# Low-weight products issued one key block later, and one product for both rotated halves of the sliding keys

## The chip, the cores and the metric

The kernel runs on one core of one Trainium2 chip. The metric is the device time of one execution in microseconds (us), from the first to the last instruction with what lies around them; it was 3167.22 us in the median of three runs. Five engines work side by side and wait for each other through semaphores: TensorE (PE: matrix products; PEld is its loading of the stationary operand), VectorE (DVE), ScalarE (ACT), GpSimd (POOL) and SyncE (SP, which starts the DMA transfers).

## The reference

Two transformer blocks run one after the other on 2048 tokens of width 1024, in float32. The parts that matter here are three attentions, each with 8 heads of width 64:

```python
# first block, heads 0-7: causal, with a forget gate
s = q @ k.T * scale + cum[q] - cum[k]; p = softmax(where(causal, s, -inf)); o = p @ v
# first block, heads 8-15: sliding window of 128 with a sink, two key heads, rotary positions
q, k = rope(q), rope(k); s = q @ k.T * scale; p = softmax(concat(where(band, s, -inf), sink)); o = p[:, :-1] @ v
# second block: 16 meta keys, and for each query its 256 best keys by an index score
s = q_lat @ c.T * scale + bias; p = softmax(where(selected, s, -inf)); o = p @ c
# rope: halves x1, x2 of a head
concat([x1 * cos - x2 * sin, x2 * cos + x1 * sin])
```

Around them stand the input projections, gates, a recurrent layer (HGRN2) beside the third attention, output projections and norms.

## The kernel before, in words

**Products in halves.** A float32 factor is split into a high and a low float16 half. A projection is three products per 128 of the width: high by high, high by low, low by high (`mm3_T`, lines 326 to 328 for a result with tokens along the free axis, `mm3_R`, lines 337 to 339, for tokens along the partitions).

**Attention.** All three attentions are built alike. Queries come in groups of 512 (`g`, four of them), keys in blocks of 128 (`j`). For one head and group, `prepare` loads operands and finds row maxima through extra score products, and `main` gives a list of steps: `block(j)` for each key block up to the diagonal, then `norm`. A block makes the scores, keys along the partitions, in a PSUM tile `pst`; `Att.weights` takes the exponential of it on ScalarE into a float32 tile `p32` (line 746), casts it to the high half `phi` on ScalarE or VectorE (lines 748 and 750) and subtracts to get the low half `plo` on GpSimd, some on VectorE (line 752). Each of these three tiles has three buffers. Then `Att.pv` is called for each 128 queries `s` of the group: the high half by the values' high part with a column of ones (line 776, 65 columns), the high half by the values' low part (line 777, 64 columns), and the low half by the values' high part (line 778). All of it accumulates in one PSUM tile `po` per head and group, which has one buffer. `norm` divides and stores. The sliding attention has two blocks per head and group; the last attention has one more, `meta`, for the 16 meta keys, with weights in the tiles `wmhi` and `wmlo`.

**Order.** `weave` lays the steps of `main` between those of the next head's `prepare`. The order of the text isn't the order on the engines: when the program is built, a planner with a model of times lays out each engine's queue, and takes what is earlier in the text first where it thinks it ready, with shifts from `tc.high_priority`. What writes to one PSUM tile stays in the order of the text. On the chip each engine then works through its queue.

**Projections of the first block.** `stream` goes through the weight blocks of `blocks1`; the heads' attention is woven in. `rotated` handles queries and keys of the sliding attention, whose weight columns are ordered so that the first halves of the heads come first. For each group of 512 tokens it makes one product for the first halves and one for the second halves (`m` rows each: 128 for four query heads, 64 for the two key heads), each in one of the two PSUM buffers `pp`, multiplies both by cosine and sine on VectorE (lines 523 and 524), combines on GpSimd (line 525), splits and stores. The work tiles `ra` have four buffers.

Of the kernel before, what the change touches and what calls it, by code (L numbers as in the profile page):

```python
# [10 lines left out]
F32 = mybir.dt.float32  # L11
# [456 lines left out]
def blocks1(K, A, h, sp, wp, er, ps, pso, fa, cum):  # L468

    nc = K.nc  # L470
# [33 lines left out]
    def rotated(kind, c0, m):  # L504
        def f(w, inv, rn):
            q, k, c, ci = (x[:, c0:c0 + 1] for x in (K.sq, K.sk, K.sc_, K.sci))
            if kind == "kb":
                angles(K, A, sp)
                norm_scale(K, wp, rn, K.hn, k)
                nc.vector.tensor_copy(K.sk[:, 1:2], k)  # L510
                inv = times(K, wp, "inv8", inv, k)
            else:
                norm_scale(K, wp, rn, times(K, wp, "hn8", K.hn, 8.0), q)
                score_scale(K, q, k, c, ci)
                inv = times(K, wp, "inv8", inv, 0.125, q)
            for g in range(NG):
                p = [ps.tile([128, 512], F32, name="pp")[:m] for _ in range(2)]
                for a in range(2):
                    mm3_T(K, p[a], w, a * m, h[g])
                tb = [table(g, a)[:m] for a in range(2)]  # L520
                for a in range(2):
                    x, y = (sp.tile([128, 512], F32, name="ra", tag="ra", bufs=4)[:m] for _ in range(2))
                    nc.vector.scalar_tensor_tensor(x, p[a], inv[:m], tb[0], op0=ALU.mult, op1=ALU.mult)  # L523
                    nc.vector.scalar_tensor_tensor(y, p[1 - a], inv[:m], tb[1], op0=ALU.mult, op1=ALU.mult)
                    nc.gpsimd.tensor_tensor(x, x, y, op=ALU.add if a else ALU.subtract)
                    store_rot(x, halves_of(K.d_qb, c0 * 4, 4, a, g * 512, 512) if kind == "qb" else
                              halves_of(K.d_kb, 0, 2, a, g * 512, 512))
        return f
# [46 lines left out]
    for kind, c0, cols in BLK1:  # L575
        n = sum(m for _, m in cols)
# [145 lines left out]
class Att:  # L722
# [46 lines left out]
        nc.scalar.copy(qa[64:66], p[64:66])  # L769
        return z  # L770

    def pv(self, o, hi, lo, v, first=False, last=False):

        nc = self.K.nc
        kw = dict(skip_group_check=True)
        nc.tensor.matmul(o, lhsT=hi, rhs=v[:, :65], start=first, stop=False, **kw)  # L776
        nc.tensor.matmul(o[:, 1:65], lhsT=hi, rhs=v[:, 65:129], start=False, stop=False, **kw)  # L777
        nc.tensor.matmul(o, lhsT=lo, rhs=v[:, :65], start=False, stop=last, **kw)  # L778

    def norm(self, po, inv, h, dst, add=None, key="on"):  # L780

# [21 lines left out]
class Swa:  # L803
# [62 lines left out]
    def main(self, g, h, ops):  # L866
        K, at = self.K, self.at
        nc = K.nc
        QA, QB, es = ops
        KA, KB, v = self.keys[g, h // 4]  # L870

        def scores(p, c, j, s, n, mask, m0):
            k, q = slice(j * 128, j * 128 + 128), slice(s * 128, s * 128 + n)
            kw = dict(skip_group_check=True)
            nc.tensor.matmul(p[:, c:c + n], lhsT=KA[:66, k], rhs=QA[:66, q], start=True, stop=False, **kw)
            nc.tensor.matmul(p[:, c:c + n], lhsT=KB[:, k], rhs=QB[:, q], start=False, stop=False, **kw)
            nc.tensor.matmul(p[:, c + m0:c + n], lhsT=K.idb, rhs=mask, start=False, stop=True, **kw)

        po = []

        def block(b):
            if b == 0:
                po.append(self.pso.tile([128, 4, 65], F32, name="spo"))
            p = self.pst.tile([128, 512], F32, name="pst")
            if b == 0:

                scores(p, 128, 4, 3, 128, K.mT2[:, :128], 0)
                if g:
                    scores(p, 0, 0, 0, 128, K.mT2[:, 128:], 0)
                scores(p, 256, 1, 0, 256, K.mT2, 0)  # L890
                prods = [(1, 4, 3), (2, 1, 0), (3, 1, 1)] + ([(0, 0, 0)] if g else [])
            else:
                scores(p, 0, 2, 1, 256, K.mT2, 0)
                scores(p, 256, 3, 2, 256, K.mT2, 0)
                prods = [(0, 2, 1), (1, 2, 2), (2, 3, 2), (3, 3, 3)]
            cc = 128 if b == 0 and g == 0 else 0
            hi, lo = at.weights(p[:, cc:], K.sci[:, h // 4:h // 4 + 1])
            for i, (c, j, s) in enumerate(prods):
                c = slice(c * 128 - cc, c * 128 - cc + 128)
                at.pv(po[0][:, s], hi[:, c], lo[:, c], v[:, j], first=b == i == 0)  # L900

        def norm():
            at.norm(po[0], K.vinvb[:, h // 4:h // 4 + 1], h, o_rows(K.d_o, D, g, 512 + h // 2 * 128), add=es, key="son")

        return [lambda: block(0), lambda: block(1), norm]


def phase_first(K, A, sk):
# [4 lines left out]
    with ExitStack() as st, ExitStack() as sr:  # L913
# [59 lines left out]
        def main(g, h, ops):  # L973
            KA, KB, QA, QB, v = ops
            po = pso.tile([128, 4, 65], F32, name="po")

            def block(j):
                s0 = max(0, j - 4 * g)
# [6 lines left out]
                if diag:  # L985
                    nc.tensor.matmul(p[:, s0 * 128:s0 * 128 + 128], lhsT=K.idb, rhs=K.mT, start=False, stop=True)
                hi, lo = at.weights(p[:, c0:], K.fci[:, h // 4:h // 4 + 1])
                for s in range(s0, 4):
                    c = slice((s - s0) * 128, (s - s0) * 128 + 128)
                    at.pv(po[:, s], hi[:, c], lo[:, c], v[:, j], first=j == 0 and s == 0, last=j == 4 * g + s)  # L990

            def norm():
                at.norm(po, K.vinv[:, h:h + 1], h, o_rows(K.d_o, D, g, h // 2 * 128), key=f"on{g % 2}")

            return [lambda j=j: block(j) for j in range(4 * g + 4)] + [norm]
# [982 lines left out]
def phase_dsa(K, A, out):  # L1978

    nc, tc = K.nc, K.tc  # L1980
    with ExitStack() as st:
# [97 lines left out]

        def main(g, h, ops, mk):  # L2080
            KA, KB, QA, QB, v, bT, bM = ops
            n = (g + 1) * 512
            po = pso.tile([128, 4, 65], F32, name="po")
            def meta():

                p = pst.tile([128, 512], F32, name="pst")
                nc.tensor.matmul(p, lhsT=KA[:66, :128], rhs=QA[:66], start=True, stop=False)
                nc.tensor.matmul(p, lhsT=KB[:, :128], rhs=QB, start=False, stop=g > 0)
                if g == 0:
                    for a in range(2):  # L2090
                        nc.tensor.matmul(p[:, :256], lhsT=jr, rhs=bM[:, a], start=False, stop=a == 1)
                hi, lo = wm
                at.weights(p[:16], K.dci[:, h // 4:h // 4 + 1], (hi, lo))
                for s in range(4):
                    c = slice(s * 128, s * 128 + 128)
                    at.pv(po[:, s], hi[:, c], lo[:, c], v[:, 0], first=s == 0)

            def block(j):
                s0 = max(0, j - 4 * g)
# [17 lines left out]
                for s in range(s0, 4):  # L2117
                    c = slice((s - s0) * 128, (s - s0) * 128 + 128)
                    at.pv(po[:, s], hi[:, c], lo[:, c], v[:, j + 1], last=j == 4 * g + s)

            def norm():
                pc = sm.tile([128, 4, 65], F32, name="pc", bufs=1)
                nc.scalar.copy(pc, po)
                at.norm(pc, K.vinv[:, h:h + 1], h, o_rows(K.d_a, D, g, h // 2 * 128), key="on")
# [209 lines left out]
```

## Time and profile before

| what | us |
|---|---|
| median of three runs | 3167.22 |
| lowest and highest | 3156.71, 3170.61 |
| profiled execution, its own time | 3170.48 |
| its span, first to last instruction | 3168.7 |
| TensorE busy in it | 2822.7 |

Times in the rows are microseconds unless marked ns. A row of a group of instructions has line, engine, operation, what it writes <- reads, shapes and count, then busy time, mean duration of one in ns, idle time of its engine just before, and what ended most of that idle time. Records of matrix products overlap, since a product's record holds the way through the array; the distance between two starts tells what one takes of the engine. TensorE's granted clock was 0.938 of the full 2.4 GHz in the mean. The first block's projections and attentions run to about 1400 us, the second block's projections and index scores to about 2240 us, and the last attention with the recurrent layer and the output projection from there to the end.

### The profile page before, as it was taken

The numbers are of one execution on the slowest core, as the hardware profiler recorded it, in microseconds if no ns is written. First come the engines' busy times: TensorE is split into PE (matmuls) and PEld (weight loads), VectorE is DVE, ScalarE is ACT, GpSimd is POOL, SyncE is SP. The second block draws the span as 40 slices with busy tenths as digits, with TensorE's granted clock in tenths as the row PEclk, the third lists the DMA queues.
The fourth block names the chain that finished last, engine by engine and source line by source line (L and its number), as shares of the span: only waits on it lengthen the run. The fifth ranks groups of instructions, "written<-read, shape, count | busy, mean of one in ns | idle before, by whom it ended". The sixth has DMA issues, their size and how long they took to land. (4 is left out here: it accounts for less than half of the span.)

```text
span 3168.7 us, 65862 instructions
## 1 busy us (share of the span) xinstructions
PE 2822.7 (89%) x25152; PEld 1858.8 (59%) x25152; DVE 2101.6 (66%) x5073; ACT 1686.9 (53%) x3058; POOL 1450.2 (46%) x1241
## 2 busy tenths in 40 slices
PE   7899999999997899999998889899678888988997
PEld 5554444477884555544445665358566566666663
DVE  7523765566678676646499699830578778888763
ACT  4423665576566655634356466321455456657763
POOL 3211446564333555534233433610456567768752
PEclk9899999999996799999999989899679989999998
DMA  6222343532235343334433532222753444443331
GB/s 235 82 87 84 105 129 111 173 95 69 79 94 167 109 142 108 124 91 157 111 97 101 160 125 73 89 91 63 182 159 102 137 133 113 118 117 110 122 97 59
DMA packets 271184, 364.28 MB, mean 115 GB/s; under 512 B 60205, under 2 KB 192033, under 8 KB 269705
## 3 DMA queue, kind: packets, MB, share of 16 engines
q1 hardware_dynamic: 270424, 359.96, 37.8%
q8 instruction: 199, 3.26, 0.4%
q14 instruction: 129, 1.05, 0.1%
q10 hardware_dynamic: 432, 0.02, 0.0%
HBM read 247.05 MB, written 112.82 MB: 114 GB/s over the span
## 5 line engine op out<-in xcount | busy, mean ns | idle before, releaser
L752 POOL TENSOR_TENSOR plo<-p,phi 128x512 f16<-128x512 f32 (+3 forms) x600 | 664.9, 1121 | 569.9 <-ACT phi L748 360.0
L748 ACT CAST phi<-p 128x512 f16<-128x512 f32 (+3 forms) x649 | 347.0, 554 | 84.2 <-PE po L778 75.1
L746 ACT ACTIVATE p<-pst,shift,dci 128x512 f32<-128x512 f32 (+4 forms) x352 | 247.4, 716 | 137.2 <-POOL plo L752 46.7
L778 PE MATMUL po<-v,plo 128*128 128x65 f16 x2176 | 270.1, 196 | 35.0 <-POOL plo L752 27.9
L776 PE MATMUL po<-v,phi 128*128 128x65 f16 x2176 | 286.4, 197 | 5.3 <-ACT phi L748 4.2
L777 PE MATMUL po<-v,phi 128*128 128x64 f16 x2176 | 285.3, 198 | 0.0
L778 PEld LDWEIGHTS <-plo 128*128 128x128 f16 x2424 | 234.7, 101 | 79.2 <-POOL plo L752 46.8
L746 ACT ACTIVATE p<-pst,shift,fci 128x512 f32<-128x512 f32 (+1 forms) x320 | 220.1, 710 | 113.1 <-PE pst L984 70.2
L963 DVE TENSOR_REDUCE mu<-p 128x1 f32<-128x512 f32 (+2 forms) x320 | 188.4, 603 | 130.1 <-PE p L959 83.3
L776 PEld LDWEIGHTS <-phi 128*128 128x128 f16 x2424 | 236.1, 100 | 48.8 <-ACT phi L748 11.4
L284 POOL TENSOR_TENSOR wlo<-wraw,whi 128x512 f16<-128x512 f32 (+3 forms) x116 | 149.9, 1310 | 216.9 <-ACT whi L283 214.0
L2058 DVE CUSTOM_DVE_ANT_0 jk<-p,mk 128x512 bf16<-128x512 f32 (+2 forms) x320 | 193.4, 604 | 80.5 <-PE p L2052 32.8
L777 PEld LDWEIGHTS <-phi 128*128 128x128 f16 x2424 | 235.6, 100 | 15.3 <-issue 1.8
L337 PE MATMUL pp<-whi,hhi 128*128 128x256 f16 (+2 forms) x824 | 235.0, 286 | 7.7 <-ACT whi L283 5.7
L339 PE MATMUL pp<-whi,hlo 128*128 128x256 f16 (+2 forms) x824 | 233.2, 285 | 4.2 <-POOL hlo L465 4.2
L338 PE MATMUL pp<-wlo,hhi 128*128 128x256 f16 (+2 forms) x824 | 234.7, 285 | 0.6 <-POOL wlo L284 0.6
L326 PE MATMUL pp<-hhi,whi 128*128 128x512 f16 (+2 forms) x496 | 190.7, 384 | 4.4 <-DVE ra L523 4.4
L328 PE MATMUL pp<-hhi,wlo 128*128 128x512 f16 (+2 forms) x496 | 190.3, 384 | 0.0
L327 PE MATMUL pp<-hlo,whi 128*128 128x512 f16 (+2 forms) x496 | 190.0, 383 | 0.0
L328 PEld LDWEIGHTS <-wlo 128*128 128x128 f16 (+2 forms) x1000 | 99.7, 100 | 122.6 <-POOL wlo L284 10.9
L326 PEld LDWEIGHTS <-whi 128*128 128x128 f16 (+2 forms) x1000 | 100.5, 101 | 120.1 <-issue 10.2
L327 PEld LDWEIGHTS <-whi 128*128 128x128 f16 (+2 forms) x1000 | 99.9, 101 | 117.3 <-issue 16.0
(666 smaller groups left out, 8933.6 us busy)
## 6 DMA issues: line engine op xcount, KB each, us to landing
wraw<-in_w_in_dram SPq DMA_DIRECT2D x88, 256.0 KB
d_z<-er SPq DMA_DIRECT2D x128, 128.0 KB
bT<-d_rb SPq DMA_DIRECT2D x32, 384.0 KB
wa<-in_w_ada_dram SPq DMA_DIRECT2D x8, 1024.0 KB
x<-in_x_dram SPq DMA_DIRECT2D x16, 512.0 KB
d_k<-ehi SPq DMA_DIRECT2D x32, 256.0 KB
d_q<-ehi SPq DMA_DIRECT2D x32, 256.0 KB
QA<-d_q SPq DMA_DIRECT2D x64, 128.0 KB
```

The costliest lines, as they stand in the source:

```text
L326: nc.tensor.matmul(ps, lhsT=whi, rhs=hhi[:, kk, :], start=kk == 0, stop=False)
L327: nc.tensor.matmul(ps, lhsT=whi, rhs=hlo[:, kk, :], start=False, stop=False)
L328: nc.tensor.matmul(ps, lhsT=wlo, rhs=hhi[:, kk, :], start=False, stop=kk == KK - 1)
L337: nc.tensor.matmul(ps, lhsT=hhi[:, kk, s], rhs=whi, start=kk == 0, stop=False)
L338: nc.tensor.matmul(ps, lhsT=hhi[:, kk, s], rhs=wlo, start=False, stop=False)
L339: nc.tensor.matmul(ps, lhsT=hlo[:, kk, s], rhs=whi, start=False, stop=kk == KK - 1)
L746: nc.scalar.activation(p, s, AF.Exp, scale=ci[:m], bias=K.shift[:m])
L748: nc.scalar.copy(hi, p)
L752: e.tensor_tensor(lo, p, hi, op=ALU.subtract)
L776: nc.tensor.matmul(o, lhsT=hi, rhs=v[:, :65], start=first, stop=False, **kw)
L777: nc.tensor.matmul(o[:, 1:65], lhsT=hi, rhs=v[:, 65:129], start=False, stop=False, **kw)
L778: nc.tensor.matmul(o, lhsT=lo, rhs=v[:, :65], start=False, stop=last, **kw)
```

## The change

Two things change. In `rotated`, where a half has 64 rows (the sliding keys), one product of 128 rows makes both halves; a copy on ScalarE brings rows 64 to 127 to a tile of partitions 0 to 63. In the attentions, `pv` is called once per block with all its products: it issues the products of the high weights for all query columns, then those of the low weights of the block before, which it finds in the list `late`, and puts its own low products there. `flush`, at the start of `norm`, issues what is left.

```diff
             for g in range(NG):
-                p = [ps.tile([128, 512], F32, name="pp")[:m] for _ in range(2)]
-                for a in range(2):
-                    mm3_T(K, p[a], w, a * m, h[g])
+                if m == 64:
+
+                    pb = ps.tile([128, 512], F32, name="pp")
+                    mm3_T(K, pb, w, 0, h[g])
+                    z = sp.tile([128, 512], F32, name="ra", tag="ra", bufs=4)[:m]
+                    nc.scalar.copy(z, pb[m:])
+                    p = [pb[:m], z]
+                else:
+                    p = [ps.tile([128, 512], F32, name="pp")[:m] for _ in range(2)]
+                    for a in range(2):
+                        mm3_T(K, p[a], w, a * m, h[g])
...
-    def pv(self, o, hi, lo, v, first=False, last=False):
+    def pv(self, prods, late):
+
 
         nc = self.K.nc
         kw = dict(skip_group_check=True)
-        nc.tensor.matmul(o, lhsT=hi, rhs=v[:, :65], start=first, stop=False, **kw)
-        nc.tensor.matmul(o[:, 1:65], lhsT=hi, rhs=v[:, 65:129], start=False, stop=False, **kw)
-        nc.tensor.matmul(o, lhsT=lo, rhs=v[:, :65], start=False, stop=last, **kw)
+        for o, hi, lo, v, first, last in prods:
+            nc.tensor.matmul(o, lhsT=hi, rhs=v[:, :65], start=first, stop=False, **kw)
+            nc.tensor.matmul(o[:, 1:65], lhsT=hi, rhs=v[:, 65:129], start=False, stop=False, **kw)
+        self.flush(late)
+        late.append(lambda: [nc.tensor.matmul(o, lhsT=lo, rhs=v[:, :65], start=False, stop=last, **kw)
+                             for o, hi, lo, v, first, last in prods])
+
+    def flush(self, late):
+        while late:
+            late.pop(0)()
...
                 hi, lo = at.weights(p[:, c0:], K.fci[:, h // 4:h // 4 + 1])
-                for s in range(s0, 4):
-                    c = slice((s - s0) * 128, (s - s0) * 128 + 128)
-                    at.pv(po[:, s], hi[:, c], lo[:, c], v[:, j], first=j == 0 and s == 0, last=j == 4 * g + s)
+                cs = lambda s: slice((s - s0) * 128, (s - s0) * 128 + 128)
+                at.pv([(po[:, s], hi[:, cs(s)], lo[:, cs(s)], v[:, j], j == 0 and s == 0, j == 4 * g + s)
+                       for s in range(s0, 4)], late)
 
             def norm():
+                at.flush(late)
                 at.norm(po, K.vinv[:, h:h + 1], h, o_rows(K.d_o, D, g, h // 2 * 128), key=f"on{g % 2}")
...
```

The sliding attention and the last one (its `meta` and `block`) are changed in the same way, with a list `late` for each head and group.

## Rows read from the trace of the kernel before

**Rows 1.** The page, part 1: busy time of each engine over the span.

```profile
PE 2822.7 (89%) x25152; PEld 1858.8 (59%) x25152; DVE 2101.6 (66%) x5073; ACT 1686.9 (53%) x3058; POOL 1450.2 (46%) x1241
```

**Rows 2.** Busy time in stretches: PE, PEld, DVE, ACT, POOL, clock, DMA share, GB/s.

```profile
430.00:505.00 75.00, 72.51 (x551) 37.68 (x552) 40.90 (x90) 39.82 (x80) 46.90 (x44) 1.00 0.37 111
...
700.00:950.00 250.00, 246.69 (x2963) 209.85 (x2961) 165.75 (x521) 156.93 (x296) 94.32 (x95) 1.00 0.28 84
...
950.00:1400.00 450.00, 396.52 (x3521) 241.47 (x3520) 301.40 (x757) 262.32 (x473) 217.40 (x175) 0.88 0.41 124
...
2240.00:3168.00 928.00, 790.47 (x9356) 567.10 (x9354) 691.36 (x1430) 542.37 (x902) 579.57 (x453) 0.92 0.41 119
```

**Rows 3.** Groups of PE by shape, 430 to 505 us: count | busy, mean ns.

```profile
L328 PE MATMUL pp<-hhi,wlo 128*64 128x512 f16 x57 | 21.7, 383 | 0.0
...
L328 PE MATMUL pp<-hhi,wlo 128*128 128x512 f16 x11 | 4.2, 379 | 0.0
```

**Rows 4.** Timeline of PE in that stretch: start us, duration us, instruction.

```profile
442.66 0.38 PE L327 MATMUL pp<-hlo,whi 128*64 128x512 f16 x1
...
446.54 0.38 PE L327 MATMUL pp<-hlo,whi 128*64 128x512 f16 x1
```

**Rows 5.** Groups of ACT over the span: the nearest copy out of PSUM.

```profile
L1857 ACT COPY kr<-y 128x512 f32<-128x512 f32 (+1 forms) x16 | 9.3, 579 | 3.9 <-PE y L1855 3.9
```

**Rows 6.** Timeline from 2849.5 us: one wait for a low half.

```profile
2848.75 2.13 POOL L752 TENSOR_TENSOR plo<-p,phi 128x512 f16<-128x512 f32 x1
...
2849.85 0.20 PE L776 MATMUL po<-v,phi 128*128 128x65 f16 x1
...
2850.93 0.20 PE L778 MATMUL po<-v,plo 128*128 128x65 f16 x1 [0.67 <-POOL plo L752]
...
2850.97 0.20 PE L776 MATMUL po<-v,phi 128*128 128x65 f16 x1
```

**Rows 7.** Groups of line 778 in 300:700, then 950:1400, then 2240:3168 (three rows).

```profile
L778 PE MATMUL po<-v,plo 128*128 128x65 f16 x425 | 50.2, 194 | 3.9 <-POOL plo L752 3.5 <-DVE plo L752 0.2
...
L778 PEld LDWEIGHTS <-plo 128*128 128x128 f16 x425 | 40.1, 99 | 12.7 <-POOL plo L752 7.4 <-issue 0.9 <-POOL ehi L481 0.4
...
L778 PEld LDWEIGHTS <-plo 128*128 128x128 f16 x570 | 56.5, 104 | 22.9 <-POOL plo L752 11.4 <-DVE plo L752 4.4 <-POOL z L1058 1.2
...
L778 PE MATMUL po<-v,plo 128*128 128x65 f16 x420 | 53.5, 200 | 7.6 <-POOL plo L752 4.5 <-DVE plo L752 1.5 <-DVE iq L224 1.2
...
L778 PE MATMUL po<-v,plo 128*128 128x65 f16 x1088 | 136.9, 197 | 23.3 <-POOL plo L752 19.7 <-DVE plo L752 3.0
...
L778 PEld LDWEIGHTS <-plo 128*128 128x128 f16 x1088 | 106.2, 102 | 42.0 <-POOL plo L752 27.7 <-DVE plo L752 4.2 <-issue 2.8
...
L778 PE MATMUL po<-v,wmlo 128*128 128x65 f16 x128 | 15.6, 194 | 3.6 <-POOL wmlo L752 3.5
```

**Rows 8.** The chain that ended last, 2242 to 3168 us, by line.

```profile
by line: issue 8.3%; POOL plo L752 4.2%; PE y L1147 4.0%; PE y L1145 4.0%; PE y L1146 3.9%; PE pst L2115 3.9%; PE pst L2103 3.8%; PE pst L2104 3.8%; DVE jk L2058 3.7%; PE p L2052 3.7%; DVE dc L1847 3.3%; DMA raw<-in_w_out_dram 2.7%; PE po L
```

**Rows 9.** Waits, over the span (three rows), then in 2240:3168 (one).

```profile
ACT phi L748 <- PE po L778: 75.1, 70, 5.2
...
ACT p L746 <- POOL plo L752: 57.0, 71, 3.6
...
POOL plo L752 <- PE po L778: 25.5, 17, 3.0
...
ACT p L746 <- POOL plo L752: 46.7, 60, 3.6
```

**Rows 10.** The page, part 5: the steps that make weights, and line 776's loads.

```profile
L752 POOL TENSOR_TENSOR plo<-p,phi 128x512 f16<-128x512 f32 (+3 forms) x600 | 664.9, 1121 | 569.9 <-ACT phi L748 360.0
L748 ACT CAST phi<-p 128x512 f16<-128x512 f32 (+3 forms) x649 | 347.0, 554 | 84.2 <-PE po L778 75.1
L746 ACT ACTIVATE p<-pst,shift,dci 128x512 f32<-128x512 f32 (+4 forms) x352 | 247.4, 716 | 137.2 <-POOL plo L752 46.7
...
L776 PEld LDWEIGHTS <-phi 128*128 128x128 f16 x2424 | 236.1, 100 | 48.8 <-ACT phi L748 11.4
```

More of the change, by code (lines that the diff above doesn't have):

```diff
@@ L877, in scores @@
             nc.tensor.matmul(p[:, c + m0:c + n], lhsT=K.idb, rhs=mask, start=False, stop=True, **kw)
-        po = []
+        po, late = [], []
         def block(b):
@@ L897, in block @@
             hi, lo = at.weights(p[:, cc:], K.sci[:, h // 4:h // 4 + 1])
-            for i, (c, j, s) in enumerate(prods):
-                c = slice(c * 128 - cc, c * 128 - cc + 128)
-                at.pv(po[0][:, s], hi[:, c], lo[:, c], v[:, j], first=b == i == 0)
+            cs = lambda c: slice(c * 128 - cc, c * 128 - cc + 128)
+            at.pv([(po[0][:, s], hi[:, cs(c)], lo[:, cs(c)], v[:, j], b == i == 0, False)
+                   for i, (c, j, s) in enumerate(prods)], late)
         def norm():
+            at.flush(late)
             at.norm(po[0], K.vinvb[:, h // 4:h // 4 + 1], h, o_rows(K.d_o, D, g, 512 + h // 2 * 128), add=es, key="son")
@@ L975, in main @@
             po = pso.tile([128, 4, 65], F32, name="po")
+            late = []
             def block(j):
@@ L987, in block @@
                 hi, lo = at.weights(p[:, c0:], K.fci[:, h // 4:h // 4 + 1])
-                for s in range(s0, 4):
-                    c = slice((s - s0) * 128, (s - s0) * 128 + 128)
-                    at.pv(po[:, s], hi[:, c], lo[:, c], v[:, j], first=j == 0 and s == 0, last=j == 4 * g + s)
+                cs = lambda s: slice((s - s0) * 128, (s - s0) * 128 + 128)
+                at.pv([(po[:, s], hi[:, cs(s)], lo[:, cs(s)], v[:, j], j == 0 and s == 0, j == 4 * g + s)
+                       for s in range(s0, 4)], late)
             def norm():
+                at.flush(late)
                 at.norm(po, K.vinv[:, h:h + 1], h, o_rows(K.d_o, D, g, h // 2 * 128), key=f"on{g % 2}")
@@ L2081, in main @@
             KA, KB, QA, QB, v, bT, bM = ops
-            n = (g + 1) * 512
+            late = []
             po = pso.tile([128, 4, 65], F32, name="po")
@@ L2093, in meta @@
                 at.weights(p[:16], K.dci[:, h // 4:h // 4 + 1], (hi, lo))
-                for s in range(4):
-                    c = slice(s * 128, s * 128 + 128)
-                    at.pv(po[:, s], hi[:, c], lo[:, c], v[:, 0], first=s == 0)
+                cs = lambda s: slice(s * 128, s * 128 + 128)
+                at.pv([(po[:, s], hi[:, cs(s)], lo[:, cs(s)], v[:, 0], s == 0, False) for s in range(4)], late)
             def block(j):
@@ L2116, in block @@
                 hi, lo = at.weights(p[:, c0:], K.dci[:, h // 4:h // 4 + 1])
-                for s in range(s0, 4):
-                    c = slice((s - s0) * 128, (s - s0) * 128 + 128)
-                    at.pv(po[:, s], hi[:, c], lo[:, c], v[:, j + 1], last=j == 4 * g + s)
+                cs = lambda s: slice((s - s0) * 128, (s - s0) * 128 + 128)
+                at.pv([(po[:, s], hi[:, cs(s)], lo[:, cs(s)], v[:, j + 1], False, j == 4 * g + s)
+                       for s in range(s0, 4)], late)
             def norm():
+                at.flush(late)
                 pc = sm.tile([128, 4, 65], F32, name="pc", bufs=1)
```

## The prediction

> **What bounds the kernel now.** I read the page's busy times first. TensorE is busy 89% of the span, its weight loads 59%, and no other engine passes 66% [rows 1]. That 89% isn't a full TensorE: a 65-column product is recorded with 0.20 us, yet the next starts 0.04 us after it (2850.93 and 2850.97, [rows 6]), so the records overlap. So I went on by stretches [rows 2]. The first projections with head attention woven in (430 to 505 us) leave the matmul engine 2.5 of 75 us; from 700 to 950 us it is idle for 3 of 250. From 950 to 1400 it is idle 53 of 450 us, and in the last attention (2240 to 3168) 138 of 928, where VectorE has 691 us of work and GpSimd 580. So TensorE is the bound up to about 950 us, and later stages hang on chains that cross engines.
>
> The wait that the change is about is seen in one block [rows 6]: GpSimd is 2.13 us in writing the low half, TensorE issues the first two high products of the block (line 776, then 777) and then stands until 2850.93 us at line 778, though the high products of the other three column groups need nothing more; they follow 0.04 us later. By stretches, the matmul engine idles at line 778 for 3.9, 7.6 and 23.3 us, and 3.6 us at the sixteen meta keys' one; the weight loads idle longer, 12.7, 22.9 and 42.0 us [rows 7]. The chain that ended last, which covers the last 926 us alone, names the subtraction that makes the low half for 4.2% of them, 39 us [rows 8].
>
> **The sliding keys.** Two 64-row products per group of 512 tokens become one of 128 rows. It removes 4 groups x 24 products = 96 matmuls and their 96 loads. A 64-row product takes as long as a 128-row one, 383 against 379 ns [rows 3], though the records overlap here too: in an unbroken run the eighteenth product after the one at 442.66 us starts at 446.54 [rows 4], so one takes 3.88 / 18 = 0.216 us of the engine. 96 x 0.216 = 20.7 us. The stretch has 2.5 us of idle TensorE, and the stage behind it 3 in 250, so what is saved moves everything behind it: I take the whole, bounds 0 (below, case D) and 20.7.
>
> It adds four copies of 64x512 out of PSUM on ScalarE. The nearest row, 128x512 out of PSUM, has 579 ns [rows 5]: 4 x 0.58 = 2.3 us on an engine that is busy 40 of 75 us there [rows 2]; priced at nothing, 2.3 us if that cover were gone. The copy waits for its group's last product; behind it on ScalarE stand exponentials and casts of the heads, and two of the group's four VectorE products now wait 0.58 us longer, hidden by the two that read the other half straight from PSUM. A product now holds one PSUM buffer instead of both, so the next group's product can begin while VectorE still reads this one; that is worth at most the 2.5 us and I count nothing. Four `ra` buffers now serve five tiles a group: the fifth takes the slot of the copy, whose last reader stands ahead of it on VectorE; nothing.
>
> **The products of the low weights.** No product and no load is added or removed. All high products of a block go first, then the low ones of the block before. In [rows 6] the six high products that stood behind line 778 would have gone at 2849.9. What it is worth lies between nothing (the next wait ends just as late) and the idle time of the loads, 12.7 + 22.9 + 42.0 = 77.6 us. An idle load costs nothing while a product still streams, so I go by the matmul engine's own idle time. Up to 1400 us I take all of it, 3.9 + 7.6 = 11.5 us. In the last attention it is 23.3 + 3.6 = 26.9 us, and of that I take half, 13.4: there GpSimd's subtraction also holds up the exponentials, which wait 46.7 us for it because the float32 weights have three buffers [rows 9], and this the change doesn't touch. So 25 us, bounds 0 and 78.
>
> Two more effects. The buffer of the high half is released by the high products alone, no longer by products that stand behind a low half; ScalarE waits 75.1 us for it, 70 times [rows 9]. I count nothing in the sum, since ScalarE is at 53% [rows 1]; it is case B. At a head's end the lows of the last two blocks now follow its last high product, at most three more products at 0.04 us [rows 6], 0.12 us a head; over 96 heads (eight, in four groups, three times) this is bounded by 12 us. I take nothing: the subtraction of the last block isn't ready sooner, and they run under it.
>
> **A rule that speaks against it.** In [rows 6] the high products that were ready waited behind line 778: products ran in the order in which they were issued. The Trainium skill, page "TensorE: Matmul & The Clock Gate", section "Part 2: What happens when you issue a matmul", says that matmuls stay in program order and that only weight loads are pulled ahead. By that rule the wait may only change its place, from the low half to the next block's high half (case C); the sum would then keep the keys' part alone.
>
> **Sum.** 20.7 + 25 = 45.7 us. The profiled execution took 3170.5 us, 3.3 above the median of the three runs; on the median that gives 3167.2 - 45.7 = 3121.5 us, 1.4% less; a profiled execution would take some 3125. I say 3121.
>
> **The cases.** A difference of about 0.5% (16 us) is what a measurement of this kernel can tell from none.
>
> A (0.50), the sum. For it speaks that the idle time at line 778 is named in every attention stage [rows 7]. Its own range has 8 to 58 us for the lows beside the keys' 20.7: 3088 to 3138.
>
> B (0.15), more than the sum: the waits of ScalarE for the high half's buffer were part of the same chain. If 40 of the 75.1 us come back too, 3121 - 40 = 3081. For it: the two waits occur in the same blocks, since a low half that is late keeps the buffer of the high half. Against: exponentials still wait for GpSimd [rows 9].
>
> C (0.13), the wait moves to the high products. Between blocks that follow each other on ScalarE lie one exponential and one cast, 0.72 + 0.55 = 1.27 us, and the low half comes 1.12 us after its high half [rows 10]: the next high half can be as late as the low half was, and behind it on TensorE are queued the lows, ready by then, and the score products that come after them, on which the next exponential waits. Then the lows give nothing and 3167 - 20.7 = 3146 stays. Against it: of the 48.8 us that loads idle at line 776 only 11.4 are put down to the cast [rows 10], so the order on TensorE mostly comes to the high products once they are ready.
>
> D (0.12), the keys' saving doesn't arrive and the lows give little: at 950 us another stage begins, whose idle time and clock of 0.88 [rows 2] show that it isn't paced by TensorE alone. With 0 to 10 us: 3157 to 3167.
>
> E (0.10), slower. The order is laid out anew by the planner, and each low half's buffer is held until the next block's high products have gone, one block longer: 928 us over 352 exponentials is 2.6 us [rows 2, 10]. There are three buffers. GpSimd waits for them 17 times now, 25.5 us, 1.5 us each [rows 9]. The gain is used up when 31 more such waits lie on the chain (45.7 / 1.5), and from 42 on the kernel is slower by over 16 us; at 47 it is 3167 - 45.7 + 70.5 = 3192. Against: a block's subtraction and its hold come to 1.12 + 2.6 us, of three buffers' 7.9.
>
> Faster by over 0.5%: A, B and most of C, 0.75. Within: the rest of C and D, 0.15. Slower: E, 0.10. The range, 3070 to 3160, takes in A, C, most of B and the low end of D; E lies outside, with the far end of B (lows at their bound of 78: 3069).
>
> **What would show it.** Right: 96 fewer products, none of 128*64 from the sliding keys; the stage behind 700 us begins some 20 us sooner; idle time of the matmul engine at line 778's successor falls from 38 us over the three stretches to under 10, and that of line 776 hardly grows; ScalarE's wait for the high half's buffer falls below 40 us. For C: the cast is named for over 30 us ahead of the high products. For D: the stage at 950 us starts sooner, but ends when it did. For E: GpSimd's wait for the low half's buffer is 70 us or more. Wrong altogether would be a last attention that takes as long as before although line 778 no longer waits: then that wait was not what set the end, and my half of it too much.

## The result, and the profile after

The changed kernel takes 3211.17 us in the median of four runs (3210.18 to 3212.24), the kernel before 3162.06 us in the median of four beside it (3156.71 to 3170.61). The ratio is 1.0152, with a 95% interval of 1.0128 to 1.0176: slower by some 49 us, where 46 us were forecast as gain.

The busy times of the page answer to [rows 1]: TensorE has the 96 products fewer, and 5.6 us less to do, in a span that is 41 us longer.

```profile
PE 2817.1 (88%) x25056; PEld 1854.7 (58%) x25056; DVE 2126.7 (66%) x5073; ACT 1684.6 (52%) x3056; POOL 1440.2 (45%) x1241
```

The windows answer to [rows 2], with the same columns.

```profile
430.00:505.00 75.00, 58.91 (x412) 30.30 (x410) 57.54 (x102) 40.52 (x81) 52.68 (x46) 0.91 0.39 117
...
700.00:950.00 250.00, 246.30 (x2961) 207.41 (x2958) 170.81 (x516) 159.34 (x298) 96.90 (x97) 1.00 0.27 82
950.00:1400.00 450.00, 383.80 (x3450) 234.99 (x3447) 300.82 (x750) 262.24 (x474) 210.50 (x172) 0.88 0.39 118
...
2240.00:3168.00 928.00, 783.49 (x9315) 567.55 (x9313) 678.10 (x1436) 543.45 (x904) 569.27 (x449) 0.90 0.42 120
```

From 430 to 505 us TensorE is busy 58.9 us where it was 72.5, and does 139 products fewer, so more than the 96 that were removed: it isn't ahead, it is idle (16.1 us of the 75). From 950 to 1400 us it does 71 products fewer than before.

The waits over the span answer to [rows 9].

```profile
POOL plo L760 <- PE po L789: 86.7, 50, 7.2
...
PEld L786 <- ACT phi L756: 48.1, 54, 5.3
...
ACT p L754 <- POOL plo L760: 39.1, 45, 3.1
```

GpSimd now waits 86.7 us for a free low-half buffer (25.5 before), and the weight loads of the high products wait 48.1 us for the cast (11.4 before, [rows 10]). The exponentials' wait for GpSimd fell from 57.0 to 39.1, and ScalarE's wait for the high half's buffer from 75.1 to 27.8, the last figure of this row of the page:

```profile
L756 ACT CAST phi<-p 128x512 f16<-128x512 f32 (+3 forms) x649 | 348.9, 554 | 40.0 <-PE po L787 27.8
```

The groups of the high products (line 786) and the low ones (line 789), from 300 to 700 us and then in the last attention, answer to [rows 7]. The last part of a row is the matmul engine's idle time just ahead.

```profile
L786 PE MATMUL po<-v,phi 128*128 128x65 f16 x396 | 41.8, 195 | 17.0 <-ACT phi L756 13.2 <-DVE on L810 3.1 <-DVE phi L758 0.6
L789 PE MATMUL po<-v,plo 128*128 128x65 f16 x390 | 31.2, 195 | 0.6 <-POOL plo L760 0.6
...
L786 PE MATMUL po<-v,phi 128*128 128x65 f16 x1088 | 115.5, 194 | 6.6 <-ACT phi L756 6.5
...
L789 PE MATMUL po<-v,plo 128*128 128x65 f16 x1088 | 86.4, 196 | 22.8 <-POOL plo L760 14.3 <-DVE plo L760 8.4
```

In the first attention the idle time has fallen ahead of the low products (3.9 to 0.6 us) and grown ahead of the high ones (3.6 to 17.0 us, 13.2 of them until the cast). In the last attention it stayed at the low ones: 22.8 us after 23.3. Added up over the three stretches of [rows 7], the meta keys and the sliding attention with them, the engine was idle 8.1 us ahead of high and 40.1 us ahead of low products before; after the change it is 37.2 and 26.7 us.

### The profile page after: what moved, and what is told of

Same layout as the page of the kernel before. It is cut to its first block, busy times and chain, and to the rows that moved or that the text cites. A ratio compares the mean times of both kernels' runs of the same rounds, so it can differ in the third digit from the quotient of the medians.

```text
span 3209.8 us, 65571 instructions
## 1 busy us (share of the span) xinstructions
PE 2817.1 (88%) x25056; PEld 1854.7 (58%) x25056; DVE 2126.7 (66%) x5073; ACT 1684.6 (52%) x3056; POOL 1440.2 (45%) x1241
## 3 DMA queue, kind: packets, MB, share of 16 engines
q1 hardware_dynamic: 270424, 359.96, 37.3%
## 5 line engine op out<-in xcount | busy, mean ns | idle before, releaser
L756 ACT CAST phi<-p 128x512 f16<-128x512 f32 (+3 forms) x649 | 348.9, 554 | 40.0 <-PE po L787 27.8
L754 ACT ACTIVATE p<-pst,shift,dci 128x512 f32<-128x512 f32 (+4 forms) x352 | 246.5, 716 | 134.0 <-PE pst L2133 54.7
L786 PE MATMUL po<-v,phi 128*128 128x65 f16 x2176 | 231.4, 196 | 33.0 <-ACT phi L756 25.3
L2077 DVE CUSTOM_DVE_ANT_0 jk<-p,mk 128x512 bf16<-128x512 f32 (+2 forms) x320 | 193.5, 605 | 96.7 <-PE p L2071 45.7
L786 PEld LDWEIGHTS <-phi 128*128 128x128 f16 x2424 | 192.9, 100 | 90.3 <-ACT phi L756 48.1
L787 PE MATMUL po<-v,phi 128*128 128x64 f16 x2176 | 231.6, 197 | 0.0
L787 PEld LDWEIGHTS <-phi 128*128 128x128 f16 x2424 | 185.1, 99 | 20.9 <-issue 3.2
L789 PE MATMUL po<-v,plo 128*128 128x65 f16 x2176 | 173.6, 196 | 24.7 <-POOL plo L760 15.2
L326 PE MATMUL pp<-hhi,whi 128*128 128x512 f16 (+1 forms) x464 | 180.3, 388 | 7.8 <-DVE ehi L346 4.4
L327 PE MATMUL pp<-hlo,whi 128*128 128x512 f16 (+1 forms) x464 | 180.1, 388 | 0.0
L328 PE MATMUL pp<-hhi,wlo 128*128 128x512 f16 (+1 forms) x464 | 179.9, 388 | 0.0
L789 PEld LDWEIGHTS <-plo 128*128 128x128 f16 x2424 | 133.1, 100 | 58.8 <-POOL plo L760 21.7
L328 PEld LDWEIGHTS <-wlo 128*128 128x128 f16 (+1 forms) x968 | 96.1, 100 | 122.1 <-POOL wlo L284 11.0
L327 PEld LDWEIGHTS <-whi 128*128 128x128 f16 (+1 forms) x968 | 96.2, 100 | 119.5 <-issue 21.9
L326 PEld LDWEIGHTS <-whi 128*128 128x128 f16 (+1 forms) x968 | 96.8, 101 | 117.6 <-ACT whi L283 9.8
```

The source lines that it names most:

```text
L326: nc.tensor.matmul(ps, lhsT=whi, rhs=hhi[:, kk, :], start=kk == 0, stop=False)
L327: nc.tensor.matmul(ps, lhsT=whi, rhs=hlo[:, kk, :], start=False, stop=False)
L328: nc.tensor.matmul(ps, lhsT=wlo, rhs=hhi[:, kk, :], start=False, stop=kk == KK - 1)
L754: nc.scalar.activation(p, s, AF.Exp, scale=ci[:m], bias=K.shift[:m])
L756: nc.scalar.copy(hi, p)
L789: late.append(lambda: [nc.tensor.matmul(o, lhsT=lo, rhs=v[:, :65], start=False, stop=last, **kw) for o, hi, lo, v, first, last in prods])
```

## The experiments

Two theories were set against each other at first. "Layout": the planner lays all queues out anew for the changed text, and that order costs what was lost. "The change itself": a removed wait comes back in a worse place, with the low halves' buffers held longer. All ratios are to the kernel before, run beside them.

| run | what is done | median us | ratio, 95% interval |
|---|---|---|---|
| e1 | keys alone | 3171.95 | 1.0016 [0.999, 1.0043] |
| e2 | lows alone | 3190.86 | 1.007 [1.0049, 1.0092] |
| e3 | highs, then lows, same block | 3205.8 | 1.0113 [1.0057, 1.017] |
| e4 | lows alone, four low buffers | 3210.52 | 1.0135 [1.0078, 1.0193] |
| p1 | lows, order held | 3169.9 | 0.9994 [0.9979, 1.001] |
| p2 | keys, order held | 3173.08 | 1.0003 [0.9987, 1.0019] |
| p3 | highs, then lows, order held | 3171.13 | 0.9997 [0.9981, 1.0012] |
| p4 | whole change, order held | 3170.08 | 0.9989 [0.9974, 1.0003] |
| p5 | keys with highs, then lows, order held | 3171.6 | 1.0002 [0.9987, 1.0017] |
| q1 | e2's layout, lows put back | 3275.79 | 1.0348 [1.033, 1.0365] |
| q2 | the change's layout, lows put back | 3287.03 | 1.0378 [1.036, 1.0396] |
| q3 | before, weave 0.5 to 0.49 | 3176.31 | 1.0033 [1.0017, 1.0048] |
| q4 | before, priority -200 to -190 | 3170.03 | 1.0004 [0.9986, 1.0023] |
| q5 | before, weave 0.3 to 0.29 | 3181.53 | 1.0037 [1.0017, 1.0058] |
| h1 | change, early order held, late new | 3177.41 | 1.0018 [0.9998, 1.0038] |
| h2 | change, early new, late order held | 3205.91 | 1.0126 [1.0092, 1.016] |
| h3 | change, new up to 680 us alone | 3176.34 | 1.0012 [0.9995, 1.0029] |
| h4 | change, new from 680 to 1400 us alone | 3203.52 | 1.0091 [1.007, 1.0113] |

**The parts alone, the planner free.** e1 has only the edit of `rotated`, e2 only those of the attentions. e3 has the high products of a block first, but its own low ones right behind, so nothing is delayed. e4 is e2 with four buffers for the low half in the first block's attentions; the last attention keeps three.

```diff
 # e3: pv and flush as in the change, but
-        self.flush(late)
         late.append(lambda: [nc.tensor.matmul(o, lhsT=lo, ...
                              for o, hi, lo, v, first, last in prods])
+        self.flush(late)
 # e4, beside the change of the attentions
+        hi, lo = (... self.pp.tile([128, 512], F16, name=x, bufs=n_) for x, n_ in (("phi", 3), ("plo", self.nlo)))
```

e1 was expected to give:

> Only the sliding keys' single product; the products of the low weights stay where they were. If the low weights' order alone is what costs (theory buffers: a low half's buffer is held a block longer and GpSimd waits; theory queue: the wait moves to the next block's high products), the 20.7 us of removed products show in full or in part: 3141 to 3155 us against some 3162. If the keys' part itself disturbs the stage up to 700 us (the attention lags by 24 us at 500 us in the changed kernel, although products were removed there), it is slower than before, 3170 to 3185.

e2 was expected to give:

> Only the low products moved behind the next block's high products; two 64-row products for the keys as before. Theories buffers and queue: it carries the whole loss, and without the 20.7 us of the keys it is slower than the changed kernel, 3215 to 3235 us. If the keys' part is what costs, it lies near the kernel before or below it, 3130 to 3175.

e3 was expected to give:

> As the lows alone, but the list is flushed behind the block's own high products: all high products of a block, then all its low ones, nothing carried into the next block. A low half's buffer is released as before, and no low product stands behind another block's high product. Theories buffers and queue: the loss is gone, and the six high products that were ready no longer wait for the low half: 3140 to 3162 us. If it is as slow as the lows alone (over 3190), the loss comes from the order being laid out anew and not from the carrying over.

e4 was expected to give:

> As the lows alone, with four instead of three buffers for the low half in the first block's attentions (the last attention has no memory for a fourth). Theory buffers: GpSimd's wait for the buffer goes down in the stretch up to 1400 us and the first block ends 10 to 30 us sooner than with the lows alone. Theory queue: the wait of the loads for the cast stays at some 40 us over the span, and the time is within 10 us of the lows alone.

The keys alone change nothing that can be measured; whether a new order hides their 20.7 us is settled by p2 below. The lows alone cost 24 us and lie between the two ranges of their expectation. But e3, which carries no low product into the next block, costs 39 us, and the fourth buffer, which brings GpSimd's wait for its buffer from 64.5 us in e2 to 37.3, makes the kernel slower still (3210.5). The times don't follow the waits that the theory of the change itself names.

**The same edits with the queues held.** To take the planner out, every engine's queue was written out: after the text of the kernel, each instruction is tied behind the one that precedes it in the order that the planner had chosen for the kernel before. Only what the edit itself moves has another place: low products behind the last high product of the next block (p1, p4) or of their own (p3, p5), the 96 products gone, the four copies behind the product that they read. In the traces of p1 to p5 ScalarE's and GpSimd's instructions come one for one in the order of the kernel before, the added copies aside, and of VectorE's 5073 all but at most eight. The kernel before itself, tied in this way, wasn't run.

```diff
+def pin(tc, nc):
+    a = np.frombuffer(zlib.decompress(base64.b85decode(ORDER)), np.int32)
+    keyed, at = engine_lists(nc), 0
+    for e in ("Pool", "DVE", "SP", "Activation", "PE"):
...
+        for k in want:
+            if last is not None:
+                tc.add_manual_dep(d[k], last, mybir.DependencyInfo(mybir.DependencyClass.NoSync, ...
+            last = d[k].name
```

p1 was expected to give:

> The lows alone, but every engine's queue is written out as it was in the kernel before; only TensorE's differs, in that a block's high products go together where its first one stood, and its low products behind the high products of the next block. Theory layout (the loss comes from the planner laying out all queues anew, the moved products themselves are worth something): the loss is gone, 3125 to 3160 us. Theories buffers and queue (the moved products themselves cost): still slower than before by 15 us or more, 3180 to 3200 us, with GpSimd's wait for the low half's buffer and the loads' wait for the cast as large as in the kernel with the lows alone (64 and 33 us).

p2 was expected to give:

> The keys alone, all queues as before; TensorE's without the 96 products, ScalarE's with the four copies behind their products. Theory layout: the 20.7 us show at least in part, 3140 to 3160 us (the queues stay as they were planned for the longer products, so what stood behind for other reasons stays). Theory that the keys' saving is hidden anyway: within 5 us of the kernel before.

p3 was expected to give:

> All queues as before, but a block's high products go together where its first one stood, and the low products keep their places: nothing is carried into the next block. Theory layout: faster than before by up to 25 us, 3140 to 3162, where the planner's own order of the same text took 3206. Theory queue: the low products still stand in front of other work, so within 5 us of the kernel before.

p4 was expected to give:

> The whole change, lows and keys, with all queues as before but for the moved and removed products and the four copies. Theory layout: the forecast sum of 45.7 us in large part, 3115 to 3150 us. Theories buffers and queue: at or over 3167 us.

p5 was expected to give:

> Keys' rotated halves from one product, every block's high products gathered ahead of its low ones, the low ones in their own block; every queue in the order of before. By the runs with the order held (0.9994, 1.0003, 0.9997, 0.9989) each theory has it at 0.997 to 1.001 (3158 to 3172 us); it is the one combination left that could beat the kernel before, which it does below 0.997.

All five medians lie within 0.11% of the kernel before, and no interval leaves 0.9974 to 1.0019. So the whole loss goes with the order of the queues. But the change in the old order gains nothing that can be measured either: p1 to p4 miss the gains that the layout theory gave them. p1 misses the loss of the other theory too; p4 meets its "at or over 3167 us" by the number alone, since the kernel before took 3171.66 us beside it. p4's windows, set beside [rows 2], show where the gain stayed (line numbers of the held kernels are some 35 higher, for the added text):

```profile
430.00:505.00 75.00, 57.55 (x445) 31.18 (x446) 45.02 (x90) 41.07 (x84) 49.41 (x44) 0.86 0.36 109
700.00:950.00 250.00, 247.58 (x2974) 210.50 (x2971) 165.62 (x523) 156.69 (x296) 94.23 (x95) 1.00 0.28 84
```

From 430 to 505 us TensorE is busy 57.6 us of 75: the 15 us that it lost are idle time, and from 700 to 950 us it does 2974 products as against 2963. The same VectorE instruction starts at 431.0 us in the kernel before and at 430.9 in p4, a later one at 701.7 and 702.1: what 96 fewer products saved is gone before 700 us. p4's waits show the other half:

```profile
POOL plo L791 <- PE po L823: 71.1, 37, 5.9
ACT p L785 <- POOL plo L791: 67.5, 72, 3.6
```

GpSimd waits 71.1 us for its buffer, 45.6 more than before, and the exponentials 67.5 us for GpSimd, 10.5 more, in a kernel that is no slower. TensorE idles 19.7 us ahead of high and 22.8 us ahead of low products, 42.5 in all; before it was 48.2. Of the 40.1 us at the low products 17.3 are gone, and the high products have 11.6 more. In p1, without the keys, the low products lose 22.4 us and the high ones gain 8.3: 14.0 us are gone from both places together, and the time is the same.

They came back elsewhere, as p4's last attention shows. One and the same VectorE instruction starts at 2241.7 us in the kernel before and at 2234.8 in p4, so the window from 2233 us to p4's end answers to the last row of [rows 2]: it has three products more, and as many instructions of VectorE, ScalarE and GpSimd. Below it stand p4's low products in that window, for which [rows 7] has 23.3 us:

```profile
2233.00:3168.10 935.10, 792.40 (x9359) 569.39 (x9356) 703.50 (x1430) 540.00 (x902) 580.07 (x453) 0.92 0.42 118
...
L823 PE MATMUL po<-v,plo 128*128 128x65 f16 x1088 | 84.4, 197 | 13.0 <-POOL plo L791 12.6
```

The wait at the low products has fallen by 10 us, yet TensorE is idle 142.7 us of 935.1 where it was 137.5 of 928.0. Ahead of the score products that serve the row maxima of the next heads it idles 7 us more.

That GpSimd waits longer isn't the work of the longer hold alone. p3 carries nothing into the next block, and has:

```profile
POOL plo L783 <- PE po L814: 64.9, 34, 5.1
...
ACT phi L779 <- PE po L813: 33.4, 20, 7.8
```

GpSimd's wait for the low half's buffer and ScalarE's for the high half's come to 98.3 us together in p3 and 100.2 in p4, and to 100.6 in the kernel before (25.5 and 75.1, [rows 9]). With the high products gathered, what ScalarE waits less GpSimd waits more; which wait turned into which wasn't followed block by block.

**The order by itself.** q1 and q2 turn it round: the queues of e2 and of the changed kernel, written out, with each block's low products right behind its own high ones. q3, q4 and q5 are the kernel before with one constant of the planner or of `weave` changed a little, so that the queues are laid out anew and hardly anything else happens. In the traces TensorE's order departs from that of the kernel before at 2297 us in q3, at 2267 in q4 and at 840 in q5.

```diff
 # q1, q2, TensorE's queue: low products of block k
-high(k) ... high(k+1) low(k)
+high(k) low(k) ... high(k+1)
 # q3: WV[1] 0.5 -> 0.49; q5: WV[0] 0.3 -> 0.29; q4: PC -200 -> -190
-WV = ((0.0, 0.3), (0.0, 0.5))
+WV = ((0.0, 0.3), (0.0, 0.49))
```

q1 was expected to give:

> All engines' queues are written out in the order that the planner chose for the lows-alone kernel (ratio 1.007), but every block's low products stand again right behind that block's own high products on TensorE; the keys are as before. The work and the place of the low products are those of the highs-then-lows kernel whose queues were held in the order of before (0.9997); only the order of the queues differs. Theory 'the new layout of the queues costs it': it stays slow, ratio 1.004 to 1.013 (3175 to 3205 us). Rival 'the low products held one block later cost it, by GpSimd's wait for its buffer': with the lows back the time falls to 0.997 to 1.002.

q2 was expected to give:

> The same with the order that the planner chose for the changed kernel (ratio 1.0152): keys' rotated halves from one product as in the change, low products again right behind their own block's high products. Theory 'layout': 1.010 to 1.018 (3192 to 3220 us). Rival 'the delay of the lows costs it': 0.997 to 1.003; something between would divide the loss between the two.

q3 was expected to give:

> The kernel before, with none of the change: one constant that says how early the side work is woven into the last attention's blocks goes from 0.5 to 0.49. No instruction is added, save that a few transposes and loads move between blocks in the text; the planner lays the queues out anew. Theory 'layout': the time moves by 0.3 per cent or more, likelier up than down (1.003 to 1.015), since the order of before is one draw that came out well. Rival 'a new layout by itself is worth nothing, the change's own instructions cost it': 0.998 to 1.002.

q4 was expected to give:

> The kernel before, with none of the change: the planner's priority offset of one kind of side work in the last attention (chunks of the other branch) goes from -200 to -190. The work is the same, instruction for instruction; only the order differs, from the last attention on. Theory 'layout': the time moves by 0.2 per cent or more, 1.002 to 1.012 or, less likely, below 0.998. Rival: 0.998 to 1.002.

q5 was expected to give:

> The kernel before, with none of the change: the constant that says how early the side work is woven into the first attention's blocks goes from 0.3 to 0.29. Theory 'any new layout of the early stages costs some': 1.002 to 1.010. Rival 'only the layout that the planner makes for the moved low products is dear': 0.998 to 1.003, as with the two constants of the last attention (1.0033 and 1.0004).

q1 and q2 miss both expectations: they are 85 and 76 us slower than the kernels whose layouts they have. In those layouts the low products stand one block later, and nothing is left between a block's high products and its low ones to fill the gap. The group of low products of q1's last attention:

```profile
L814 PE MATMUL po<-v,plo 128*128 128x65 f16 x1088 | 87.2, 197 | 92.6 <-POOL plo L783 81.1 <-DVE plo L783 10.8
```

92.6 us of idle time, where the kernel before has 23.3 [rows 7]. Without the delay these layouts are slower still, but by a stall that is new, so the two runs price neither the layout nor the delay by itself. That the delay costs nothing in the order of before is what p1 and p4 show. The small constants say more of the layout, and against the theory in its broad form: a new layout of the same kernel costs 0.04 to 0.37%, not 1.5. Of these only q5 lays out anew what lies before 1400 us. e1's new order, from some 440 us on, costs 0.16%, with 1 in its interval. So these few draws show no sign that the order of before is a rare stroke of luck, though none is faster; the layouts made for the edited attentions cost 0.7 to 1.5%.

**Where the loss lies.** h1 and h2 are the whole change with the order of before in one half of the program, and the order that the planner chose for the changed kernel in the other; the border is the end of the second projections, at about 1400 us. h3 and h4 divide the early half at about 680 us:

```diff
 # order of the queues:  to 680 us   680 to 1400 us   from 1400 us
 # p4                    before      before           before
-# the change            new         new              new
+# h1                    before      before           new
+# h2                    new         new              before
+# h3                    new         before           before
+# h4                    before      new              before
```

The queue of a single engine was not exchanged.

h1 was expected to give:

> The whole change, with every queue written out: up to the end of the second projections in the order of before (as in the kernel with both parts and its order held, 0.9989), and from there on, the last 1800 us with the last attention in them, in the order that the planner chose for the changed kernel. Theory 'the loss is divided between the layouts of the two halves': 1.002 to 1.008 (3173 to 3192 us), as the changed kernel lost 33 of its 41 us before 1400 us and the lows-alone kernel lost 18 of its 25 in the last attention. Rival 'it sits in the early half alone': 0.998 to 1.001. Rival 'it sits in the late half alone': 1.012 to 1.017.

h2 was expected to give:

> The mirror image: the whole change, its first 1400 us in the order that the planner chose for the changed kernel, the rest in the order of before. Theory 'divided': 1.007 to 1.013 (3189 to 3208 us). Rival 'early half alone': 1.012 to 1.017. Rival 'late half alone': 0.998 to 1.001. The two runs' losses together should come to the 1.4 to 1.6 per cent of the changed kernel, if a layout's price in one half doesn't depend on the other.

h3 was expected to give:

> The whole change with every queue written out: the instructions that the order of before issues up to about 680 us (the keys' products and the first heads of the first attention) stand among themselves in the order that the planner chose for the changed kernel, all the rest in the order of before. Theory 'the stage around 1000 us carries the loss', where the new layout leaves TensorE 156 us busy in 200 and the held one 168: 0.998 to 1.003. Rival 'the stretch up to 680 us carries it', where the changed kernel is 25 us late at 500 us: 1.008 to 1.013.

h4 was expected to give:

> The whole change: the instructions up to about 680 us in the order of before, those from there to the end of the second projections (about 1400 us) in the order that the planner chose for the changed kernel, the stages behind in the order of before. Theory 'the stage around 1000 us carries the loss': 1.008 to 1.013 (3195 to 3215 us). Rival 'the stretch up to 680 us carries it': 0.998 to 1.003. If both runs come out dear or both cheap, the price is not one stage's, but comes of how the two meet.

The loss is not divided evenly: 1.26% go with the early half, 0.18% with the late one, together 1.44 of the 1.52. By its ranges h1 lies just between 'early half alone' and 'divided', and h2 in both. Within the early half h4 has 0.91%, h3 0.12. So the changed kernel loses most of it between 680 and 1400 us. e2, e3 and e4 lose theirs elsewhere, though no half of them was held. Counted by TensorE's records, e2 and e4 are 6 and 7 us behind the kernel before at the 15700th product (2210 us there) and 24 and 32 us at the 24000th (3031 us), so most of it goes in the last attention; e3 is 20 us behind at the 4000th (651 us) already and 35 at the 24000th.

Counted by TensorE's records, the 7400th starts at 947.6 us in p4 and at 950.4 in h4, the 9400th at 1199.1 and 1226.0: 2000 products, of nearly the same kinds, take 251.5 us in the order of before and 275.6 in the new one, 24 of the loss of some 30. The window from 950 to 1250 us, first p4, then h4:

```profile
950.00:1250.00 300.00, 260.88 (x2364) 161.36 (x2363) 221.42 (x585) 182.89 (x334) 143.59 (x119) 0.87 0.46 136
```

```profile
950.00:1250.00 300.00, 245.35 (x2215) 149.45 (x2212) 209.75 (x544) 174.92 (x321) 139.49 (x117) 0.85 0.45 134
```

TensorE is idle 54.7 us there with the new order and 39.1 with the old one. The waits of the same window, first p4, then h4 (line 804 writes a next head's row maxima, line 807 transposes them on TensorE):

```profile
POOL plo L791 <- PE po L823: 6.1, 4, 4.2
...
PE p L807 <- DVE zrow L804: 3.2, 3, 1.8
```

```profile
POOL plo L791 <- PE po L823: 22.8, 8, 5.1
...
PE p L807 <- DVE zrow L804: 14.1, 7, 4.2
```

TensorE stands 11 us longer at the row maxima of the next head, work that the change doesn't touch, because it comes to them before VectorE has made them. The changed kernel and h2 have the same two waits (14.3 and 22.4 us, 14.1 and 20.3), the kernel before and h3 have not (2.2 and 5.2, 3.5 and 6.3). So the waits go with the slow order in these six kernels. e2 has both as well (12.9 and 17.5 us) and e1 8.8 us of the first, and they lose little in this window (2272 and 2324 products, 2310 in the kernel before). q5, which has none of the change, has 12.3 us of the first, does 2247 products and loses 0.37% in all. That the waits are the cause is argued only. In e4 and e3 neither is there (3.7 us and none, 3.0 and 2.8), and they do 2313 and 2444 products in this window; they lose their 43 and 39 us elsewhere.

## Why the prediction was wrong

**The sum priced the edits in the old order, and there it was wrong by the whole sum.** p4 is that very case, and its ratio of 0.9989 stands for 3.5 us where 45.7 were summed; by the interval it can be anything from 8 us less to 1 us more.

- *The keys, 20.7 us.* The 96 products went, as counted, and nothing else came. The step that failed is "the stretch has 2.5 us of idle TensorE ..., so what is saved moves everything behind it". A stretch with a busy TensorE is not one that TensorE alone paces: in p2 it idles 19.3 of the 75 us, in small waits for seven things (low halves 4.8, row maxima 3.7, casts 2.9, queries 2.4, exponentials 2.1, score maxima 2.1, and 1.4 for `norm`, which reads the sums out of PSUM). Before, the window had 2.4 us of such waits. So of the 20.7 us some 17 came back as idle time and the rest as longer records at a lower clock (last section). Case D had the outcome of p4, at 0.12, and with a later place: the saving was gone before 700 us, not at 950.
- *The lows, 25 us.* The wait at line 778 fell up to 1400 us as forecast (3.9 to 0.6 and 7.6 to 0.9 us in the changed kernel), but the high products took over in part, which was case C: its sign, over 30 us of the cast ahead of high products, came to 27 us by the matmul engine and 48.1 us by the loads. In p4 the low products lose 17.3 us of idle time and the high ones gain 11.6. The rule of the Trainium skill that was weighed ("TensorE: Matmul & The Clock Gate", section "Part 2: What happens when you issue a matmul", products stay in program order) points that way, and these rows agree with it. The step that failed is taking the idle time at one line for time that the kernel would get back: what the high products didn't take came back ahead of other products. In the last attention the changed kernel has 22.8 us left where I had taken half of 23.3 as gain.
- *Case B.* ScalarE's wait for the high half's buffer did fall, from 75.1 to 27.8 us (29.1 in p4), and bought nothing.

**The term that set the sign was left out: the order.** Taking 25 us from a few waits, I left all other instructions where they were. The text says that the planner lays out the queues anew, and I used that only to bring in case E. E forecast 3192 us and its sign came true: GpSimd waits 86.7 us for its buffer, where 70 were asked for. But its price of 1.5 us a wait is refuted, since p4 has 71.1 us of that wait and is no slower, and e4 has 37.3 and is. Nor does the wait need the longer hold that E names: p3 has 64.9 us without it. What costs is the order chosen for the moved products, mostly from 680 to 1400 us (h4).

**What was right.** 96 products fewer; ScalarE's wait under 40 us; the copies, priced at nothing, took 582 ns each in p2 and p4, and VectorE waited for one of them once, 1.7 us. What was named as "wrong altogether", that the wait at the low products didn't set the end, is what p4 shows: 13.0 us of it in the last attention after 23.3, and a last attention that is no shorter.

**What stays open.** Which instruction's new place makes TensorE late between 950 and 1250 us, what in their orders costs e2, e3 and e4 their time, and why the orders made for the edited attentions cost more than those of q3 to q5. Whether an order made for the change could be faster than the kernel before wasn't found out. No version here beats the kernel before.

## What to carry to other kernels

Where a planner lays out the queues, an edit has two prices, that of its instructions and that of the order it gets; hold the order once and measure the first by itself, and change a constant a little to see how far the second moves without any edit. An engine that is 97% busy in a stretch isn't proved to be its pace: ask which chains would end within a few us behind each removed product. A long wait that disappears is worth only the distance to the next one, and the next one can stand anywhere: at the two places that were watched idle time fell by 5.7 us in p4 and by 14.0 in p1, and neither kernel is faster. So look at the engine's idle time over the whole stage and not at the lines that the edit names.

## What was unexpected of the hardware

With 96 products fewer the clock fell too: from 430 to 505 us TensorE was granted 1.00 of its clock before [rows 2] and 0.84 in the mean in p2. The clock first fell there at 436 us, to 1.2 from 2.4 GHz, behind 3.7 us of idle time at the next head's row maxima.

```profile
430.00:505.00 75.00, 55.72 (x431) 30.50 (x430) 45.10 (x95) 41.46 (x85) 48.28 (x43) 0.84 0.34 104
```

The projections' products of that stretch, one of three such groups:

```profile
L331 PE MATMUL pp<-hhi,whi 128*128 128x512 f16 x31 | 13.5, 436 | 0.0
```

A record has 436 ns in the mean where it had 383 [rows 3]. Over the 92 products of the three groups (13.5 + 13.0 + 12.9 = 39.4 us, as against 92 x 0.383 = 35.2) that is some 4 us of the 20.7 given back by the clock on these products, an estimate, as the records overlap. Over all products the bound is 75 x (1.00 - 0.84) = 12 us, had TensorE been busy all the time.
